# A hybrid streaming encoder step on one core: the gated projection with tokens on partitions, its result turned by VectorE, and VectorE and ScalarE held in source order beside it

## The chip, the core and the metric

The kernel runs on one core of a Trainium2 chip. A core has a matrix engine (TensorE, PE in the profile), a vector engine (VectorE, DVE), an activation engine (ScalarE, ACT), a general engine (GpSimd, POOL) and a queue that mostly issues transfers (SyncE, SP). Each engine takes its instructions in one fixed order and waits, at an instruction, until everything that this instruction needs is there; what stands behind it waits too. The metric is the device time of one execution in microseconds (us); three runs of the kernel before gave 1998.6, 1998.66 and 1998.87.

## The reference, cut to what matters

One layer of an encoder is applied to 384 frames in float32: 256 frames of a new stream and 8 running streams of 16 frames. With `h = rmsnorm(x)` and one combined projection `proj = h @ w_in` it computes

```
u  = glu_in[:, :1024] * sigmoid(glu_in[:, 1024:])          # gated input of the convolution
A  = swish(layernorm(causal_dwconv(u, 31 taps))) @ conv_pw_out
q, k = rmsnorm(q), rmsnorm(k) ; logf = log_sigmoid(f_logit)
B  = softmax(q k^T * scale + cumsum(logf) bias, causal) v @ w_att_out    # 8 heads of 128
x  = x + (sigmoid(gA) * A + sigmoid(gB) * B) @ w_out
x  = x + (silu(causal_dwconv(g, 3 taps)) * u2) @ w_down , [g | u2] = rmsnorm(x) @ w_up
```

It returns both outputs, the new keys, values and forget logs, and the new convolution states (the last 30 rows of `u` for each stream, the last two of `g`).

## The kernel before

**Products.** All large products run on PE in a split form: each float32 operand is written as `hi` (rounded to the matmul's input type) plus `lo` (the rest), and hi·hi, hi·lo and lo·hi are added up. The activations are split once. The weights are streamed by `fetch` through three raw buffers of 128 x 2 x 512, and each raw tile is split by `split_rows` (lines 146 to 149): ScalarE casts `hi` (L148), then VectorE subtracts `lo` (L149). There are three `hi`/`lo` pairs, so the ScalarE cast for weight tile n can start only when PE has read tile n-3 for the last time. `ahead` asks for the splits two or three tiles before PE needs them.

**Jobs and units.** `gemm` runs a list of jobs. One pass of its inner loop, called a *unit* here, is one 128-deep slice of the contraction; a weight tile serves two units. A job of kind "B" has the tokens on partitions: three token blocks, each 128 x 512 in PSUM, nine matmuls a unit (L250 to L252). A job of kind "A" has features on partitions: four blocks of 128 features by 384 tokens, twelve matmuls a unit (L245 to L247). Only the gated projection (4 jobs of 16 units, units 0 to 63 in what follows) is of kind "A". At the end of each unit `tick` runs work that was put off by `after` and then one step of each side generator; so side work is tied to units in the source.

**The stages.** Values, queries and keys come first, with RMS norms; then the gated projection, beside which the attention of all heads and the first part of the 31-tap convolution run; then the two gate projections (8 jobs of kind "B", 128 units), beside which the rest of the convolution and its layer norm run; then the projections of attention and convolution, `w_out`, and the feed-forward part (up and down), which takes from about 800 us to the end.

**Beside the gated projection.** For head h, `attention` puts these steps behind unit 5+6h+off: off 1 `head_operands` (VectorE turns the past keys, `kTs`, L611), off 4 `head_scores` (PE; then VectorE adds the bias and takes maxima, `pr`, L636; ScalarE exponentials L639, VectorE reciprocals, ScalarE scaling L641), off 9 `head_probs` (PE transposes; copies by ScalarE and VectorE), off 12 `head_out` (PE; copies `on` L665 and `attT` L670 by VectorE), off 14 `head_last` (PE transposes `on`). `conv` yields one step a unit: for channel block c the states are loaded, `fill` builds the shifted input `ext` (16 units apart for load, 3 before the first tap), and each of 31 taps is one VectorE instruction (L752 for the first, L754 for the rest) that works in place in `ut`. Blocks follow each other every 17 units, beginning 24 units after unit 0. `fill` also has PE transpose two pieces of `ut` (L740, L741), which ScalarE copies and SP stores as the new state; the first tap overwrites `ut`, so it waits for these transposes. The evacuation of a gated job (`glu_evac`) multiplies PSUM by the token scale `rs1b` laid along the free axis (L706, L710), takes the sigmoid on ScalarE and multiplies on GpSimd (L711).

**What sets the order.** PE's order is the source's. The other engines' order is made when the program is built, by a planner that models times and takes, of what is ready, what comes first in the source; `tc.high_priority(offset)` moves a piece of work forward by so many instructions: 150 for splits (`SPLIT_AHEAD`), 250 for attention steps (`ATT_AHEAD`), 400 for evacuations (`EVAC_AHEAD`), nothing for the convolution. `queued` chains an instruction behind the last one so chained on its engine. The result is one fixed list for each engine, whatever the chip then does.

## Time and profile before

| | us |
|---|---|
| median of three runs | 1998.66 |
| the profiled execution: its time | 1998.56 |
| its span in the profile | 1996.7 |
| gated projection: first to last of its matmuls | 214.6 to 384.7 |
| gates and what follows until 646 us | 261.2 |
| PE busy in the span | 1986.5 |

A row of a group gives line, engine, operation, tiles, shapes, count, then busy time and mean duration, then the idle time of the engine in front of these instructions and who ended it. A row of the timeline gives start and duration in us, then the same; where several instructions are merged, the count stands at the end. Matmuls are pipelined: each lasts longer than the distance to the next, so the pace is read from starts, and a wait of PE shows as a gap between starts.

### The profile page before, as it was taken

The page shows a single profiled execution, that of the slowest core. Times are in us where ns is not written, and L with a number is a line of the kernel's source. Part 1 is how long each engine was busy: PE and PEld are TensorE (multiplying, and loading weights), DVE is VectorE, ACT ScalarE, POOL GpSimd, SP SyncE. Part 2 cuts the span into 40 slices and gives each one's busy share as a digit, 9 for nine tenths or more (in the row PEclk, how much of TensorE's full clock was granted, in tenths as well). Part 3 has the DMA queues.
Part 4 walks back from the last instruction along what each step waited for, and adds up shares of the span by engine and source line. Part 5 has one row for each costly group of instructions (what it writes and reads, how often), then busy time and mean ns, then how long its engine had stood idle before and what let it go on. Part 6 is the DMA issues. An engine that isn't in the chain of part 4 may idle for free.

```text
span 1996.7 us, 24449 instructions
## 1 busy us (share of the span) xinstructions
PE 1986.5 (99%) x9383; PEld 1676.0 (84%) x9383; DVE 1305.3 (65%) x1908; ACT 743.2 (37%) x1077; POOL 89.5 (4%) x216
## 2 busy tenths in 40 slices
PE   9999999999999999999999999999999999999999
PEld 9888999888888888888888888888888888888887
DVE  4455889788755487676867683377673376638663
ACT  5535354433334433344333432233332233323321
POOL 1000011100000000000000000010000000000000
PEclk9999999999999999999999999999999999999999
DMA  6564767444443334534344443444433444343443
GB/s 184 149 188 117 216 154 161 141 140 131 130 129 124 128 125 163 165 122 137 119 137 126 129 134 129 129 126 127 136 129 132 132 118 137 128 133 120 138 158 106
DMA packets 209254, 275.98 MB, mean 138 GB/s; under 512 B 55878, under 2 KB 96729, under 8 KB 209129
## 3 DMA queue, kind: packets, MB, share of 16 engines
q1 hardware_dynamic: 208817, 273.85, 46.0%
q8 instruction: 73, 1.20, 0.3%
q0 software_dynamic: 288, 0.57, 0.1%
q14 instruction: 44, 0.36, 0.1%
q10 hardware_dynamic: 32, 0.01, 0.0%
HBM read 266.98 MB, written 7.86 MB: 138 GB/s over the span
## 4 chain that ended last, share of the span: by engine, by line
PE 96%; DVE 2%; DMA 1%; issue 0%; SPq 0%; ACT 0%; DVEq 0%; ACTq 0%
PE acc L252 20%; PE acc L250 20%; PE acc L251 20%; PE misc L252 10%; PE misc L251 10%; PE misc L250 10%; PE acc L245 2%; PE acc L247 2%; PE acc L246 2%; DVE lo L149 1%; DMA raw<-in_w_in_dram 0%; DVE mixT L267 0%; DVE ut L754 0%; DMA vc<-in_cache_v_dram 0%; DMA bs<-c_dr 0%
## 5 line engine op out<-in xcount | busy, mean ns | idle before, releaser
L149 DVE TENSOR_TENSOR lo<-raw,hi 128x1024 fp32r<-128x1024 f32 (+2 forms) x481 | 580.5, 1207 | 530.7 <-ACT hi L148 526.8
L148 ACT CAST hi<-raw 128x1024 fp32r<-128x1024 f32 (+2 forms) x481 | 496.3, 1032 | 970.1 <-PE misc L252 841.1
L250 PE MATMUL acc<-hi,xg 128*128 128x512 f32 x704 | 274.9, 390 | 0.0
L252 PE MATMUL acc<-hi,xg 128*128 128x512 f32 x704 | 273.9, 389 | 0.0
L251 PE MATMUL acc<-lo,xg 128*128 128x512 f32 x704 | 273.9, 389 | 0.0
L250 PE MATMUL acc<-hi,hT 128*128 128x512 f32 (+1 forms) x512 | 193.0, 377 | 0.5 <-ACT hT L297 0.5
L252 PE MATMUL acc<-hi,hT 128*128 128x512 f32 (+1 forms) x512 | 190.4, 372 | 0.2
L251 PE MATMUL acc<-lo,hT 128*128 128x512 f32 (+1 forms) x512 | 190.3, 372 | 0.0
L250 PEld LDWEIGHTS acc<-hi,xg 128*128 128x128 f32 x704 | 132.1, 188 | 28.4
L754 DVE SCALAR_TENSOR_TENSOR ut<-ext,cw,ut 128x384 f32<-128x384 f32 x240 | 151.9, 633 | 6.0
L252 PEld LDWEIGHTS acc<-hi,xg 128*128 128x128 f32 x704 | 132.1, 188 | 27.5
L251 PEld LDWEIGHTS acc<-lo,xg 128*128 128x128 f32 x704 | 132.2, 188 | 27.1
L252 PE MATMUL misc<-hi,xg 128*128 128x512 f32 x352 | 137.0, 389 | 0.0
L250 PE MATMUL misc<-hi,xg 128*128 128x512 f32 x352 | 137.0, 389 | 0.0
L251 PE MATMUL misc<-lo,xg 128*128 128x512 f32 x352 | 136.9, 389 | 0.0
L250 PE MATMUL acc<-hi,act 128*128 128x512 f32 x352 | 136.9, 389 | 0.0
L251 PE MATMUL acc<-lo,act 128*128 128x512 f32 x352 | 136.9, 389 | 0.0
L252 PE MATMUL acc<-hi,act 128*128 128x512 f32 x352 | 136.9, 389 | 0.0
L267 DVE STREAM_TRANSPOSE extf<-tok 32x384 f32<-32x384 f32 x176 | 100.3, 570 | 30.9 <-ACT tok L988 28.2
L267 DVE STREAM_TRANSPOSE uT<-tok 32x384 f32<-32x384 f32 x176 | 100.3, 570 | 29.7 <-ACT tok L988 26.9
L250 PEld LDWEIGHTS acc<-hi,hT 128*128 128x128 f32 x512 | 96.2, 188 | 16.1 <-ACT hT L297 1.0
L252 PEld LDWEIGHTS acc<-hi,hT 128*128 128x128 f32 x512 | 96.1, 188 | 15.7 <-DVE hT L298 0.7
(325 smaller groups left out, 3133.8 us busy)
## 6 DMA issues: line engine op xcount, KB each, us to landing
raw<-in_w_up_dram SPq DMA_DIRECT2D x176, 512.0 KB
raw<-in_w_in_dram SPq DMA_DIRECT2D x96, 512.0 KB
raw<-in_w_down_dram SPq DMA_DIRECT2D x88, 512.0 KB
raw<-in_w_in_dram SPq DMA_DIRECT2D x64, 256.0 KB
raw<-in_w_out_dram SPq DMA_DIRECT2D x32, 512.0 KB
raw<-in_w_att_out_dram SPq DMA_DIRECT2D x16, 512.0 KB
raw<-in_conv_pw_out_dram SPq DMA_DIRECT2D x16, 512.0 KB
raw<-in_w_in_dram SPq DMA_DIRECT2D x23, 344.0 KB
```

The lines of the kernel that those rows point to most:

```text
L148: queued(nc.scalar.copy(hi[:, k, :o], raw[:, k, :o]), first)
L149: queued(tt(lo[:, k, :o], raw[:, k, :o], f(hi[:, k, :o]), op=ALU.subtract), first)
L245: mm(o, hi[:, kk, s], ah, start=st, stop=False)
L246: mm(o, hi[:, kk, s], al, start=False, stop=False)
L247: mm(o, lo[:, kk, s], ah, start=False, stop=sp)
L250: mm(o, ah[:, s], hi[:, kk, :n], start=st, stop=False)
L251: mm(o, ah[:, s], lo[:, kk, :n], start=False, stop=False)
L252: mm(o, al[:, s], hi[:, kk, :n], start=False, stop=sp)
L267: nc.vector.transpose(put(a, slice(32 * b, 32 * b + 32)), src[32 * a:32 * a + 32, b])
L754: stt(o, v, wc, o, op0=ALU.mult, op1=ALU.add)
```

## The change: a gated projection with tokens on partitions

Kind "A" goes. The gated jobs become like all others, with 256 gate and 256 value columns in one 512-wide block. `glu_evac` then works by token block: one sigmoid on ScalarE straight from PSUM with the token scale as its scale, and one VectorE instruction that scales the value half and multiplies; the rows go to a new tile `ur`. `glu_done` turns `ur` into `ut` by VectorE transposes of 32 x 192, sixteen a job, four in each of the last unit of the job and the three after it. The new states are stored straight from `ur` by two transfers; the PE transposes, copies and small stores in `fill` go, and so do `rs1b`, its diagonals and its matmuls.

From the start of the gated projection to its end, every VectorE and ScalarE instruction that goes through the new `InOrder` wrapper is chained in source order (`chained`), but the splits and the evacuations are left free. The attention priority goes; the reciprocals of a head become one instruction a unit later (`head_scale`); key loads move two heads ahead, bias loads are issued by GpSimd instead of SP and with the value loads stand eight units behind the head's start. The convolution begins two units later. At the very start the first sample loads go to ScalarE's queue and the second `x_chunk` stands ahead of the second half of the first split; at the end the last output block is added and stored in two halves.

```diff
-CONV_FIRST, CONV_LAG = 24, 17
+CONV_FIRST, CONV_LAG = 26, 17
-SPLIT_AHEAD, ATT_AHEAD, EVAC_AHEAD = 150, 250, 400
+SPLIT_AHEAD, EVAC_AHEAD = 150, 400
...
+    class InOrder:
...
+                d = op(*a, **kw)
+                if chained:
+                    queued(d)
+                return d
...
     def split_rows(hi, lo, raw, o, k):
         first = in_first()
-        queued(nc.scalar.copy(hi[:, k, :o], raw[:, k, :o]), first)
+        held, chained[:] = chained[:], []
+        queued(act.copy(hi[:, k, :o], raw[:, k, :o]), first)
         queued(tt(lo[:, k, :o], raw[:, k, :o], f(hi[:, k, :o]), op=ALU.subtract), first)
+        chained[:] = held
...
-                    if j["kind"] == "A":
-                        o = ps[m][:, :NT]
-                        mm(o, hi[:, kk, s], ah, start=st, stop=False)
-                        mm(o, hi[:, kk, s], al, start=False, stop=False)
-                        mm(o, lo[:, kk, s], ah, start=False, stop=sp)
...
         split_rows(hi, lo, first, V_COLS[0][0][1], slice(0, 1))
         x_chunk(0)
         warm_up(FILL)
+        x_chunk(1)
         split_rows(hi, lo, first, V_COLS[0][0][1], slice(1, 2))
-        x_chunk(1)
...
     def load_b(h):
-        nc.sync.dma_start(bs[:, 0:P], c_dr[h, 0:P].partition_broadcast(P))
+        nc.gpsimd.dma_start(bs[:, 0:P], c_dr[h, 0:P].partition_broadcast(P))
...
+            for off, step in ((1, head_operands), (3, next_keys), (4, head_scores), (5, head_scale), (8, next_rest),
+                              (9, head_probs), (12, head_out), (14, head_last)):
...
     def glu_evac(g):
-        def ev(m, ps):
-            if m < 2:
-                tt(sgb[m][:], ps[:, :NT], rs1b[:], op=ALU.mult)
-                nc.scalar.activation(sgb[m][:], sgb[m][:], AF.Sigmoid)
-            else:
-                tt(u, ps[:, :NT], rs1b[:], op=ALU.mult)
-                nc.gpsimd.tensor_tensor(u, u, sgb[m - 2][:], op=ALU.mult)
+        def ev(t, ps):
+            sgb = p_att.tile([P, 256], F32, tag="sgb", bufs=2, name="sgb")
+            act.activation(sgb[:], ps[:, 0:256], AF.Sigmoid, scale=rs1[:, t:t + 1])
+            stt(ur[:, t, 256 * g:256 * (g + 1)], ps[:, 256:512], rs1[:, t:t + 1], sgb[:], op0=ALU.mult, op1=ALU.mult)
+    def glu_done(g):
+            for b in range(4):
+                after(b, lambda b=b: blocks(ur[:, :, 256 * g:256 * (g + 1)], by_feature(ut[:, 2 * g:2 * g + 2]), [b]))
...
         def fill(c):
-            tr(ps[:, :P], ut[:, c, 2 * P:], ident[:])
-            tr(ps[:32, P:2 * P], ut[:, c, 224:256], ident[:])
-            nc.scalar.copy(su[:, 0, :], ps[:, :P])
...
+    chained.append(True)
+    gemm([job(16, ha, glu_evac(g), done=glu_done(g)) for g in range(4)], [att_steps, conv_steps])
     drain(att_steps)
+    chained.clear()
...
-                tt(ys, ps[:], ys, op=ALU.add)
+                parts = [(0, 512)] if not last or n < 3 or t < 2 else [(0, 256), (256, 256)]
```

## The prediction

> **What bounds the kernel now.** I read the page first, then the pace of the matmuls, then stages by windows, and last the timeline around each wait of PE.

> ```profile
> span 1996.7 us, 24449 instructions
> PE 1986.5 (99%) x9383; PEld 1676.0 (84%) x9383; DVE 1305.3 (65%) x1908; ACT 743.2 (37%) x1077; POOL 89.5 (4%) x216
> PE 96%; DVE 2%; DMA 1%; issue 0%; SPq 0%; ACT 0%; DVEq 0%; ACTq 0%
> ...
> 214.61:384.84 170.23, 167.73 (x1192) 161.55 (x1191) 140.47 (x300) 77.89 (x146) 17.72 (x23) 0.99 0.64 164
> 384.84:646.00 261.16, 261.01 (x1160) 215.55 (x1160) 192.24 (x272) 97.71 (x131) 10.17 (x17) 1.00 0.46 133
> ...
> 215.68 0.33 PE L245 MATMUL acc<-hT,hi 128*128 128x384 f32 x1
> 225.21 0.33 PE L246 MATMUL acc<-hT,hi 128*128 128x384 f32 x1
> 1984.65 0.39 PE L250 MATMUL acc<-hi,act 128*128 128x512 f32 x1
> 1991.91 0.39 PE L252 MATMUL misc<-hi,act 128*128 128x512 f32 x1
> ```

> PE is the bound: the chain is PE for 96%. The window rows (length, then busy time of PE, PEld, DVE, ACT, POOL) are the gated projection and the gates with what follows until the layer norm. In the first VectorE is busy 140 of 170 us, in the second 192 of 261: it is the engine with the least room, and where its work stands in a bad order PE will wait for it. The pace of PE: 55 steps of 384 columns take 9.53 us, 0.1733 each; 32 steps of 512 take 7.26, 0.2269 each. One unit is 12 x 0.1733 = 2.08 us before and 9 x 0.2269 = 2.04 us after; a weight tile (two units) is 4.08 us.

> PE really waits once in the gated projection:

> ```profile
> 349.72 1.04 ACT L148 CAST hi<-raw 128x1024 fp32r<-128x1024 f32 x1 [1.47 <-PE acc L246]
> 350.80 1.22 DVE L149 TENSOR_TENSOR lo<-raw,hi 128x1024 fp32r<-128x1024 f32 x1 [1.26 <-ACT hi L148]
> 351.94 1.24 DVE L611 STREAM_TRANSPOSE kTs<-kc 128x1024 f32<-128x1024 f32 x1
> 353.23 0.64 PE L630 MATMUL misc<-kTs,qz 128*32 128x128 f32 x16 [2.50 <-DVE kTs L611]
> ...
> 354.46 0.52 PE L245 MATMUL acc<-hT,hi 128*128 128x384 f32 x1
> 357.34 0.52 PE L245 MATMUL acc<-hT,hi 128*128 128x384 f32 x1
> ```

> This is the pattern on which the whole forecast rests. The planned order put a split in front of something that PE needs at once. The split's buffer came free only when PE ended the unit (L246), ScalarE cast 1.08 us until VectorE could start, VectorE subtracted 1.14, then turned the keys, and PE stood 2.50 us. After it ten matmuls came 0.32 apart instead of 0.173: 1.5 more. This stop cost 4.0.

> **The change part by part.** *Gains.* (a) Matmuls of the gated jobs: 768 x 0.1733 = 133.1 become 576 x 0.2269 = 130.7: -2.4. (b) The state transposes leave PE:

> ```profile
> 403.02 0.39 PE L252 MATMUL misc<-hi,hT 128*128 128x512 f32 x1
> 403.25 0.27 PE L740 MATMUL misc<-ident,ut 128*128 128x128 f32 x1
> ...
> 403.70 0.40 PE L251 MATMUL acc<-lo,hT 128*128 128x512 f32 x1
> ```

> From 403.02 to 403.70 stand two ordinary steps, 0.45; the pair adds 0.23, eight pairs -1.8. (c) The `rs1b` matmuls, six records like these: -0.5 (0 to -0.8). (d) The stop above has its cause in an order that is planned anew: -4.0. (e) Start:

> ```profile
> 1.32 0.46 SPq L104 DMA_DIRECT2D xs<-in_x_sample_dram  x1
> 7.34 0.48 ACT L148 CAST hi<-raw 128x344 fp32r<-128x344 f32 x1 [1.58 <-DMA raw<-in_w_in_dram]
> 8.36 0.42 PE L250 MATMUL acc<-hi,hT 128*128 128x344 f32 x1 [0.46 <-ACT hT L297]
> ```

> PE waits for the second block of `hT`, which stands on ScalarE behind a cast that waits for a transfer; now it stands ahead, and two sample issues of 0.46 no longer sit ahead of that transfer on SP. I take -0.8, between 0 (the third weight tile, which is late anyway, gives it back) and -1.3. (f) The last add (0.69 us for 512 columns) and its store in halves: -0.2, 0 to -0.5. Sum of gains -9.7: 1998.6 - 9.7 = 1988.9.

> *Costs in the gated projection.* The prices are these rows (a 32 x 192 transpose is not in the trace: 0.38 by the line from 0.434 for 256 elements to 0.58, the step of 6 in 3.48, for 384; 0.29 if half of 0.58):

> ```profile
> L731 DVE STREAM_TRANSPOSE ext<-sc 128x256 f32<-128x256 f32 x4 | 1.7, 434 | 1.5 <-DMA sc<-in_state_conv_dram 1.4
> 771.59 3.48 DVE L267 STREAM_TRANSPOSE mixT<-sgA 32x384 f32<-32x384 f32 x6
> L665 DVE COPY on<-misc 128x128 f32<-128x128 f32 x8 | 2.3, 285 | 6.0 <-PE misc L663 6.0
> L670 DVE COPY attT<-misc 128x256 f32<-128x256 f32 x8 | 3.3, 419 | 0.5 <-PE misc L669 0.5
> L640 DVE RECIPROCAL mx<-mx 128x1 f32<-128x1 f32 x24 | 3.5, 150 | 2.5 <-ACT pr L639 2.5
> L641 ACT ACTIVATE pr<-pr,mx 128x256 f32<-128x256 f32 x16 | 8.0, 503 | 7.2 <-DVE mx L640 5.6 <-DVE mx L638 1.4
> 290.71 1.28 ACT L707 ACT_TABLE_LOAD   x1
> 294.27 1.05 ACT L707 ACTIVATE sgb<-sgb 128x384 f32<-128x384 f32 x2 [2.27 <-DVE sgb L706]
> 338.98 0.38 PE L659 MATMUL misc<-vt,pT 128*128 128x128 f32 x2
> 340.42 0.39 PE L669 MATMUL misc<-pT,vt 128*128 128x128 f32 x2
> ```

> In the changed program's built order I looked, on VectorE, for instructions that cannot start before PE ends some unit and stand ahead of one that PE needs right then. There are four.
> A, unit 19: ahead of head 0's `on` copy, which PE needs as soon as unit 19 ends, stand the split of tile 12 (its buffer is freed by unit 19), one reciprocal and four transposes of `ur`: 1.08 + 1.14 + 0.15 + 4 x 0.38 + 0.28 = 4.2 us of waiting.
> B, unit 31, the end of gated job 1: ahead of head 2's `on` copy stand the three evacuations of that job and the split of tile 16. ScalarE does two sigmoids of 0.5 and the cast of 1.05, VectorE the split 1.14, the third evacuation 0.42, a reciprocal, a tap 0.65 and the copy: 4.7. The table load (1.28) need not be added: at 290.71 it ran ahead of the wait, as here; if it does not, 6.0.
> C, unit 49: between the end of job 2 (unit 47) and head 5's `on` copy VectorE has three evacuations 1.26, a split 1.14, seven transposes 2.7, two taps 1.3, a reciprocal and the copy, behind a sigmoid: 7.3. PE has two units and the output matmuls of head 5 (338.98 to 340.6, 1.6): 5.7. Wait 1.6, up to 3 if the third exponential, now behind the sigmoids and a table load, holds the reciprocal.
> D, unit 53: the rest of the same lag meets the copy of head 6's probabilities that `head_out` needs, 1.3 by the same count, 0 to 3.
> A to D 11.8 (8 to 16). Slow matmuls after a stop, as after 353.23: 1.5 each for A and B, 3.0 (0 to 6). Together +14.8.
> [...]

> *Cost beside the gates.* Here the chain is off and taps are free. Before, each block's first tap waited for PE's transposes of `ut`, and this held VectorE to PE's units:

> ```profile
> 408.89 1.22 DVE L149 TENSOR_TENSOR lo<-raw,hi 128x1024 fp32r<-128x1024 f32 x1
> 410.03 3.23 DVE L754 SCALAR_TENSOR_TENSOR ut<-ext,cw,ut 128x384 f32<-128x384 f32 x5
> 413.18 1.22 DVE L149 TENSOR_TENSOR lo<-raw,hi 128x1024 fp32r<-128x1024 f32 x1
> 414.31 2.57 DVE L754 SCALAR_TENSOR_TENSOR ut<-ext,cw,ut 128x384 f32<-128x384 f32 x4
> 416.81 1.22 DVE L149 TENSOR_TENSOR lo<-raw,hi 128x1024 fp32r<-128x1024 f32 x1
> 417.94 3.89 DVE L754 SCALAR_TENSOR_TENSOR ut<-ext,cw,ut 128x384 f32<-128x384 f32 x6
> 421.75 1.22 DVE L149 TENSOR_TENSOR lo<-raw,hi 128x1024 fp32r<-128x1024 f32 x1
> ...
> 438.70 0.48 DVE L752 TENSOR_SCALAR ut<-ext,cw,col 128x384 f32<-128x384 f32 x1 [2.02 <-PE misc L741]
> ```

> A split with 5, 4, 6 taps takes 4.29, 3.63, 4.94 us: 1.01 + 0.655 for each tap. With five, VectorE already loses 0.2 us a tile to PE's 4.08, and makes it good in the pause of 2.02 that the transposes force. After the change no such pause is left. The built order packs taps without a break: between the splits of tile 39 and tile 71 stand 175 taps and 5 fills, 5.5 a tile. That is 32 x 1.01 + 175 x 0.655 - 5 x 0.14 (first taps are shorter) + 5 x 0.37 = 148 us, against 32 x 4.08 = 131 on PE. The splits come free two units before use, less cast and subtraction: 4.08 - 2.2 = 1.9 of slack. So PE loses 148 - 131 - 1.9 = 15 us there, a few tenths to 1.5 at each tile (12 if VectorE enters this stretch ahead, 20 if GpSimd's sums slow taps: 3 taps took 2.88 instead of 1.96 beside GpSimd). Later, with the taps done, nothing is given back: PE cannot run faster.

> ```profile
> 295.91 2.88 DVE L754 SCALAR_TENSOR_TENSOR ut<-ext,cw,ut 128x384 f32<-128x384 f32 x3
> ```

> Work that I cost at nothing: the copies and sigmoids of ScalarE (78 of 170 us busy); the bias loads, asked for eight units, over 21 us, ahead of their add, and GpSimd's queue behind them, which loses eight products; SP, which loses the 32 issues of the bias loads (four a head) and 14 small stores. If a bias load is late, `pr` waits and with it all of VectorE, chained.
> Sum: 1988.9 + 14.8 + 15 = 2018.7, so 2019. The profiled execution, 1998.56, is 0.1 from the median, 1998.66; no correction. Three runs lie within 0.3 us, so 0.2% (4 us) is ample for telling a change.

> **The rivals.** *Faster, 1989 (chance 0.14):* the lists bind less than I think. If the split buffers are free earlier than a tile's last matmul, A and B shrink to the sums without cast and split, and if a tile's VectorE work stays below 4.08 us (under 4.7 taps a tile instead of 5.5) the gates cost nothing. All gains stay. Against it: the stop at 350.35 is exactly this pattern, with its length.
> *Only one of the two stretches, 2004 (0.09):* VectorE enters the gates so far ahead that the lag never reaches PE, or the stops A to D are hidden.
> *A clock that falls again and again, 2031 (0.05):* small waits at every tile beside the gates bring the 0.32 pace back; eight times 1.5 is +12. Against it: waits of 0.3 to 0.5 elsewhere (8.36) show no such run.
> *Bias loads late, 2033 (0.05):* eight heads at 1.8 us. [...]

> **How the numbers follow.** The forecast, both stretches, has 0.67 and runs from 2008 (A to D 8, no slow clock, gates 12) to 2031 (16 + 6 + 20). The range for 8 in 10 takes in the second rival: 2002 to 2032. Faster by over 0.2%: 0.14. Within: the bottom of the second rival, 0.02. Slower: 0.84.

> **What would show it.** Right: PE gaps of about 4 us behind unit 19 and unit 31, ended by `on`; slow matmuls after each; none at head 7's keys; beside the gates PE waits ended by `lo`, and VectorE near 95% busy until the last tap, some 60 us earlier than before in units. Steps (a) and (b) show as 0.2269 and no L740 rows. Wrong: if VectorE is idle beside the gates, or a gap of PE ends with `pr` behind a bias transfer.

## The result, and the profile after

The changed kernel takes 2017.46 us (median of five runs, 2016.52 to 2018.93) against 1998.6 us before in the same series: 1.0099 times as long, 95% interval 1.0086 to 1.0113. The forecast was 2019, so the total was met, but not its parts: the gated projection lost nearly twice what was counted, and the gates lost almost nothing.

The top of the page of the changed kernel, with the shares of the chain that ended last:

```profile
span 2015.6 us, 24006 instructions
PE 1989.6 (99%) x9169; PEld 1651.6 (82%) x9169; DVE 1312.7 (65%) x1950; ACT 739.6 (37%) x1063; POOL 101.8 (5%) x240
PE 88%; DVE 9%; issue 2%; ACT 0%; DMA 0%; SPq 0%; DVEq 0%; ACTq 0%
```

VectorE does nearly the same amount of work as before (1312.7 us against 1305.3), and yet it now ends 9% of the chain instead of 2%. Windows say where. A row is a stretch, its length, the busy time of PE, PEld, DVE, ACT and POOL, and the granted clock; first the changed kernel (gated projection, gates), then the gates of the kernel before, whose gated projection stands in the prediction:

```profile
212.40:403.98 191.58, 173.51 (x994) 138.89 (x993) 137.38 (x301) 78.87 (x142) 23.13 (x41) 0.95 0.62 149
403.98:668.76 264.78, 263.95 (x1167) 217.73 (x1165) 205.34 (x317) 95.87 (x123) 12.88 (x17) 1.00 0.46 133
```
```profile
384.84:649.74 264.90, 264.75 (x1176) 218.64 (x1176) 195.98 (x278) 101.43 (x135) 10.17 (x17) 1.00 0.45 132
```

The gated projection took 170.23 us before and takes 191.58: 21.35 more, with PE idle for 18 us of the stage (191.58 less 173.51) and its clock at 0.95. The gates take 264.78 against 264.90. The projection starts 2.2 us earlier than before (212.40 against 214.61), and what follows the gates is the same within 0.2 us. So the loss lies in one stage. The waits of PE in it, by line, engine that ended them, sum, number and longest:

```profile
PE misc L688 <- DVE on L89: 9.1, 3, 4.4
PE misc L634 <- DVE pz L89: 5.0, 2, 3.2
PE misc L632 <- DVE attT L89: 3.2, 1, 3.2
PE misc L638 <- DVE qz L89: 0.8, 1, 0.8
```

(L89 is the wrapper through which every VectorE instruction now goes, so tiles tell them apart; L688 is the transpose of `on` in `head_last`, L632 and L634 are the second and third score product of a head, L638 its product with the past keys.) The wait behind unit 19, which the prediction called A, in the timeline:

```profile
259.57 0.39 PE L264 MATMUL acc<-hi,hT 128*128 128x512 f32 x1
259.99 1.04 ACT L89 CAST hi<-raw 128x1024 fp32r<-128x1024 f32 x1 [4.65 <-PE acc L264]
261.07 1.22 DVE L89 TENSOR_TENSOR lo<-raw,hi 128x1024 fp32r<-128x1024 f32 x1 [2.60 <-ACT hi L89]
262.21 0.17 DVE L89 RECIPROCAL mx<-mx 128x3 f32<-128x3 f32 x1
262.41 1.52 DVE L89 STREAM_TRANSPOSE ut<-ur 32x192 f32<-32x192 f32 x4
263.95 0.29 DVE L89 COPY on<-misc 128x128 f32<-128x128 f32 x1
264.38 0.30 PE L688 MATMUL misc<-ident,on 128*128 128x128 f32 x1 [4.43 <-DVE on L89]
```

Read it downwards: PE ends the unit, only then may ScalarE cast into the freed buffer, VectorE has stood idle for 2.60 us in front of the subtraction that needs the cast, and the 0.29 us copy that PE waits for stands behind all of it. 4.43 was measured, 4.2 was forecast. The second kind of wait was not foreseen. Unit 33, in the same view:

```profile
309.04 0.70 PE L632 MATMUL misc<-qt,attT 128*128 128x256 f32 x2
309.67 1.13 DVE L89 STREAM_TRANSPOSE ut<-ur 32x192 f32<-32x192 f32 x3
310.83 1.23 DVE L89 TENSOR_TENSOR lo<-raw,hi 128x1024 fp32r<-128x1024 f32 x1
312.09 0.37 DVE L89 STREAM_TRANSPOSE ut<-ur 32x192 f32<-32x192 f32 x1
312.47 0.29 DVE L89 COPY pz<-misc 128x128 f32<-128x128 f32 x1
312.91 0.76 PE L634 MATMUL misc<-qt,attT 128*128 128x128 f32 x2 [3.17 <-DVE pz L89]
```

The score product at L634 reads nothing that `pz` holds. It waits for a place to write: PSUM holds three `misc` tiles, a head's scores want all three, and the last of them still held probabilities of the head before, which VectorE copies out as `pz`.

### The profile page after: what moved, and what is told of

It reads as the page before. It is cut to its first block, busy times and chain, and to the rows that moved or that the text cites. A ratio compares the mean times of both kernels' runs of the same rounds, so it can differ in the third digit from the quotient of the medians.

```text
span 2015.6 us, 24006 instructions
## 1 busy us (share of the span) xinstructions
PE 1989.6 (99%) x9169; PEld 1651.6 (82%) x9169; DVE 1312.7 (65%) x1950; ACT 739.6 (37%) x1063; POOL 101.8 (5%) x240
## 4 chain that ended last, share of the span: by engine, by line
PE 88%; DVE 9%; issue 2%; ACT 0%; DMA 0%; SPq 0%; DVEq 0%; ACTq 0%
PE acc L262 20%; PE acc L263 20%; PE acc L264 20%; PE misc L264 9%; PE misc L262 9%; PE misc L263 9%; DVE ut L89 5%; DVE lo L89 3%; DVE mixT L89 0%; DVE sgA L89 0%; ACT hi L89 0%; PE misc L638 0%; PE misc L307 0%; PE misc L676 0%; DMA xs<-in_x_prompt_dram 0%
## 5 line engine op out<-in xcount | busy, mean ns | idle before, releaser
L89 DVE TENSOR_TENSOR lo<-raw,hi 128x1024 fp32r<-128x1024 f32 (+2 forms) x481 | 579.9, 1206 | 533.0 <-ACT hi L89 528.9
L89 ACT CAST hi<-raw 128x1024 fp32r<-128x1024 f32 (+2 forms) x481 | 495.7, 1031 | 961.2 <-PE misc L264 834.6
L262 PE MATMUL acc<-hi,hT 128*128 128x512 f32 (+1 forms) x704 | 272.9, 388 | 0.0
L263 PE MATMUL acc<-lo,hT 128*128 128x512 f32 (+1 forms) x704 | 267.9, 381 | 1.1 <-DVE lo L89 1.1
L264 PE MATMUL acc<-hi,hT 128*128 128x512 f32 (+1 forms) x704 | 267.6, 380 | 0.0
L263 PEld LDWEIGHTS acc<-lo,hT 128*128 128x128 f32 x704 | 133.8, 190 | 24.4 <-DVE lo L89 2.2
L262 PEld LDWEIGHTS acc<-hi,hT 128*128 128x128 f32 x704 | 133.7, 190 | 24.4 <-issue 2.1
L264 PEld LDWEIGHTS acc<-hi,hT 128*128 128x128 f32 x704 | 133.6, 190 | 23.5
L89 DVE SCALAR_TENSOR_TENSOR ut<-ext,cw,ut 128x384 f32<-128x384 f32 x240 | 138.2, 623 | 0.8
L89 DVE STREAM_TRANSPOSE extf<-tok 32x384 f32<-32x384 f32 x176 | 100.3, 570 | 30.9 <-ACT tok L89 28.2
```

What stands on the lines that cost most here:

```text
L89: d = op(*a, **kw)
L262: mm(o, ah[:, s], hi[:, kk, :n], start=st, stop=False)
L263: mm(o, ah[:, s], lo[:, kk, :n], start=False, stop=False)
L264: mm(o, al[:, s], hi[:, kk, :n], start=False, stop=sp)
```

## The experiments

The theories. *Theory 1*: PE loses time where a VectorE copy that it needs, as an operand or because the copy empties a PSUM tile, stands in the built list behind splits and transposes. *Theory 2*: the stage simply holds too much VectorE work. *Theory 3*: a convolution tap costs more when it reads what the tap just before it wrote. *Theory 4*, formed on the way: beside the gates PE loses by how densely the list is packed. Ratios are to the kernel before.

| run | time, us | ratio (95%) | gated projection, us | gates, us |
|---|---|---|---|---|
| before (1997.5 to 1998.6 in four series) | 1998 | 1 | 170.2 | 264.9 |
| changed | 2017.46 | 1.0099 (1.0086 to 1.0113) | 191.6 | 264.8 |
| e1, transposes spread | 2007.31 | 1.0049 (1.0033 to 1.0066) | 180.8 | 264.6 |
| e2, one PSUM tile less | 2009.0 | 1.0058 (1.0043 to 1.0073) | 183.1 | 264.7 |
| e3, not chained | 2002.93 | 1.0029 (1.0018 to 1.0040) | 178.8 | 263.4 |
| e4, bias by SP | 2019.55 | 1.0111 (1.0096 to 1.0126) | 191.2 | 264.7 |
| e5, taps in runs | 2015.45 | 1.0088 (1.0073 to 1.0104) | 191.5 | 262.3 |
| e6, splits in order | 2009.31 | 1.0056 (1.0040 to 1.0070) | 184.5 | 264.8 |
| e7, all places | 1995.5 | 0.9989 (0.9980 to 0.9997) | 164.9 | 267.8 |
| e8, e7 with free splits | 2007.73 | 1.0052 (1.0039 to 1.0066) | 180.5 | 263.7 |
| e9, e7 and e5 | 1993.56 | 0.9978 (0.9969 to 0.9987) | 165.6 | 265.0 |
| e10, e7 with queued taps | 1990.85 | 0.9966 (0.9954 to 0.9979) | 164.7 | 263.1 |

The last column needs one correction. In e7 to e10 twelve small matmuls of the layer norm come behind the end of the gates instead of in front of it, in e5 six. What follows the gates takes 1348.9 to 1349.1 us in e7 to e10 and 1347.6 in e5, against 1346.8 in the changed kernel; so some 2.0 and 0.8 us are to be added to their gates in a comparison.

**e1: the transposes of `ur` spread.**

```diff
-                after(b, lambda b=b: blocks(ur[...], by_feature(ut[...]), [b]))
+                after(2 * b, lambda b=b: blocks(ur[...], by_feature(ut[...]), [b]))
```

> Edit against the changed kernel: the four quarters of a job's ut transposes come two units apart instead of one. Same work on every engine, other places in VectorE's list. Theory 1 (places in the list: PE loses time where a copy that it or its PSUM buffers need stands behind splits and transposes): counted along the new built list with the durations of the trace, the wait behind unit 19 falls from 4.6 to about 2.8 us and so ends without its stretch of slow clock (about 1.7), the two waits at unit 33 lose 2 us in all, that at unit 51 some 2.5, and small ones of 0.5 to 1 come at the other heads: 5 to 7 us less, 2011 to 2013. Theory 2 (VectorE simply has too much work in this stage, 64 transposes of 0.37 us more, and PE pays for the sum wherever it stands): 2017, as the changed kernel.

10.2 us less than the changed kernel, with the same instructions. The waits of PE in e1:

```profile
PE misc L688 <- DVE on L89: 7.5, 3, 3.4
PE misc L634 <- DVE pz L89: 2.5, 4, 1.9
```

A is now 2.7 us instead of 4.4, and the waits of the score products fall from 8.2 us to about 3. Theory 2 alone can't explain the loss: the work is the same. The count was too careful by 4 us: the wait at unit 33, counted at about 1.2, came out at 0.15, and its half-clock stretch vanished too (the clock of the stage is 0.98 instead of 0.95); that behind A stayed against the count.

**e2: two score products in one PSUM tile.**

```diff
-        s1 = misc_tile()
-        mm(s1[:, :2 * P], qh[:, P:2 * P], kh[:, 0:2 * P], start=True, stop=True)
+        s1 = s0[:, P:]
+        mm(s0[:, P:3 * P], qh[:, P:2 * P], kh[:, 0:2 * P], start=True, stop=True)
```

> Edit against the changed kernel: the first two score products of a head (128 and 256 columns) share one PSUM tile, so a head asks for two of the three misc tiles at that place and not three. Theory 1 with the PSUM ring (the waits of 3.3 us at unit 33 and of 3.4 and 2.2 at unit 51 are waits for a misc tile that VectorE must empty first): these three go or move to the on copy of the same head; counted along the built list about 7 us less, near 2010, and 2008 if the clock keeps its pace there. If these waits had another cause (the query rows themselves, the keys, the bias), they stay: 2017.

As counted by theory 1. The waits of PE in e2:

```profile
PE misc L688 <- DVE on L89: 11.8, 3, 4.4
PE misc L680 <- DVE mx L89: 1.0, 1, 1.0
```

No wait of L632 or L634 is left: those 8.2 us were waits for a PSUM tile. VectorE's list had not become faster, and a part of the lag comes back at the next copy that PE needs (`on` 11.8 instead of 9.1 us).

**e3: the order not enforced.**

```diff
-    chained.append(True)
     gemm([job(16, ha, glu_evac(g), done=glu_done(g)) for g in range(4)], [att_steps, conv_steps])
```

> Edit against the changed kernel: the source order of VectorE and ScalarE beside the gated projection is not enforced; the planner places everything, the rest of the change stays. Theory 1: the list is another one and so are the waits; counted along it there are eight waits of 1 to 4.7 us, most of them now for a split that comes late (units 32 to 47) and none behind unit 19: about 8 us less than the changed kernel, 2009 to 2011, still slower than before. Rival (the enforced order alone is the loss): all waits go, and the gains stay: 1989 to 1992. Theory 2 (amount of work): 2017.

14.5 us less than the changed kernel and still slower than before; the count was 7 us too high. The planner's list makes other waits, for splits (0.5 us of the first row falls at the kernel's start, the rest in this stage):

```profile
PE acc L263 <- DVE lo L89: 7.6, 4, 3.6
PE acc L262 <- ACT hi L89: 1.2, 2, 0.7
```

VectorE is busy 159.8 us inside this shorter stage of 178.8 us, against 137.4 of 191.6 in the changed kernel: more work there and less time, which speaks against theory 2 once more.

**e4: bias loads issued by SP again.**

```diff
-        nc.gpsimd.dma_start(bs[:, 0:P], c_dr[h, 0:P].partition_broadcast(P))
+        nc.sync.dma_start(bs[:, 0:P], c_dr[h, 0:P].partition_broadcast(P))
...
```

> Edit against the changed kernel: SP issues the bias loads again, in the same places. Theory 1: no gain, 2017 to 2019 (SP then stands in front of weight loads, and the first heads' scaling comes a little later). [...]

Not faster: 1.0111 against 1.0099, with intervals that overlap. So GpSimd's issues don't explain the loss; nor does the profile of the changed kernel put any wait of PE or VectorE in this stage down to a bias load.

**e5: taps in runs of one block.** From unit 65 on, a window of eight steps gives eight taps of one block, then eight of the next, and the taps are queued:

```diff
+                d = stt(o, v, wc, o, op0=ALU.mult, op1=ALU.add)
+            if not chained:
+                queued(d)
...
+        for t in range(39, 7 * CONV_LAG + CW, 8):
+            for c in range(8):
+                for i in range(8):
+                    step(c, t + i)
```

> Edit against the changed kernel: from the end of the gated projection on, the convolution's taps are queued in runs of eight of one block, where the changed kernel alternates between two blocks; the same taps, operands and results. Theory 3 (a tap that reads the ut rows that the instruction just before it wrote starts later; that is why a tap took 0.654 us from start to start before and 0.529 after): by the built order 112 of 138 neighbouring taps beside the gates are then of one block, and these show 0.65, the others 0.53; PE loses nothing more, because the planner spreads the taps thinner and ends them some 55 us later: 2016 to 2019. Rival (GpSimd's traffic, the state copies or PE's transposes of ut made taps slow before, and these are gone): all taps stay at 0.53.

The pitch of taps between two splits: five taps of the changed kernel, where two blocks alternate, then four taps of one block in e5.

```profile
433.16 2.73 DVE L89 SCALAR_TENSOR_TENSOR ut<-ext,cw,ut 128x384 f32<-128x384 f32 x5
435.81 1.22 DVE L89 TENSOR_TENSOR lo<-raw,hi 128x1024 fp32r<-128x1024 f32 x1
```
```profile
472.76 2.57 DVE L89 SCALAR_TENSOR_TENSOR ut<-ext,cw,ut 128x384 f32<-128x384 f32 x4
475.25 1.22 DVE L89 TENSOR_TENSOR lo<-raw,hi 128x1024 fp32r<-128x1024 f32 x1
```

From tap to tap the median is 0.529 us in the changed kernel and 0.653 in most of e5's gates; where the changed kernel has one block left (from 560 us) it shows 0.654 too. In four taps only the last, in front of the split, costs 0.53: 3 x 0.653 + 0.53 is the 2.49 from 472.76 to 475.25. Theory 3 holds and its rival falls: the order alone makes the price. That it is the reading of `ut`, and not of another tile that neighbours of one block share, is the nearest explanation and was not separated. PE lost nothing by it, and the time came out just under the forecast: the gates became 2.5 us shorter, 0.8 of which returns behind them. The planner spread the taps until 623 us, and no wait for a split is left beside the gates.

**e6: the splits in source order too.**

```diff
-        held, chained[:] = chained[:], []
         queued(act.copy(hi[:, k, :o], raw[:, k, :o]), first)
         queued(tt(lo[:, k, :o], raw[:, k, :o], f(hi[:, k, :o]), op=ALU.subtract), first)
-        chained[:] = held
```

> Edit against the changed kernel: the splits too are held in source order beside the gated projection (there the split for a weight tile is asked for two tiles ahead, at a unit by which its buffer is free). Theory 1: the wait behind unit 19 falls from 4.6 to about 1 us, since no split stands there any more; the waits that come from the third evacuation at unit 31 (3.9) and from the transposes in front of the score tiles (3.1 at unit 33, 2.7 and 3.5 at 49 to 51) stay: 4 to 8 us less, 2009 to 2013. Theory 2 (amount of work): 2017.

8.2 us less, as counted. The waits of PE in e6 (its score products are L630 and L632, its transpose of `on` L686):

```profile
PE misc L632 <- DVE pz L89: 6.9, 3, 3.5
PE misc L686 <- DVE on L89: 3.6, 1, 3.6
PE misc L630 <- DVE attT L89: 2.4, 2, 1.6
```

A is gone, which was the split's; that at unit 31 and those for PSUM tiles stay.

**e7: every place changed, no instruction.** To e6 it adds:

```diff
-ATT_FIRST = 5
-CONV_FIRST, CONV_LAG = 26, 17
+ATT_FIRST = 4
+CONV_FIRST, CONV_LAG = 30, 17
...
-            ... (4, head_scores), (5, head_scale), ... (14, head_last)):
+            ... (5, head_scores), (6, head_scale), ... (15, head_last)):
...
-                after(b, lambda b=b: blocks(...
+                after(2 + 3 * b, lambda b=b: blocks(...
```

> Edit against the changed kernel: the same instructions in other places. Splits in source order too; a head starts a unit earlier but asks for its scores at offset 5 and for its last transpose at 15; the quarters of the ut transposes come 2, 5, 8 and 11 units behind the job; the convolution begins four units later. Theory 1: counted along the built list no wait of PE over 0.4 us is left beside the gated projection, so the 19.5 us of stops and the 8 to 9 of slow clock of the changed kernel go and its gains stay, less about 1 us for a later end of the convolution: 1990, from 1988 to 1993, below the kernel before. Theory 2: the work is the same, so 2010 to 2017. [...]

The gated projection takes 164.89 us, 5.3 less than before the change and 26.7 less than in the changed kernel, with a clock of 1.00 throughout. That is theory 1: the longest wait of PE left in the stage is 0.74 us. But the time is 1995.5, outside the forecast of 1988 to 1993: the gates take 3.0 us more than in the changed kernel, 5.0 with the correction above. Their window in e7, and then the only wait of PE in its first 182.9 us:

```profile
377.13:644.92 267.79, 264.55 (x1154) 215.53 (x1153) 207.50 (x313) 95.20 (x124) 11.20 (x17) 1.00 0.46 131
```
```profile
PE acc L261 <- DVE lo L89: 3.2, 7, 0.6
```

Seven waits for a split, each up to 0.6 us: a shape that the prediction had described for the changed kernel. VectorE is busy there for 174.7 of the 182.9 us.

**e8: e7 with the splits left free.**

```diff
+        held, chained[:] = chained[:], []
         queued(act.copy(hi[:, k, :o], raw[:, k, :o]), first)
         queued(tt(lo[:, k, :o], raw[:, k, :o], f(hi[:, k, :o]), op=ALU.subtract), first)
+        chained[:] = held
```

> Edit against e7: only the splits are left free again, as in the changed kernel; all else is as in e7. Theory 1: the planner then puts splits ahead of copies and exponentials that PE needs, as in the changed kernel; counted along the list there are six waits of 0.7 to 4.1 us, 11 to 12 us together: 2001 to 2004. If the splits' places don't matter, as e7.

12.2 us more than e7. The difference was counted as 11 to 12, from an e7 at 1990; as e7 itself came out at 1995.5, the forecast of 2001 to 2004 was missed. The waits of PE in e8, and the longest of them in the timeline:

```profile
PE misc L662 <- ACT pr L89: 6.6, 4, 3.7
PE misc L688 <- DVE on L89: 3.9, 1, 3.9
```
```profile
262.48 1.04 ACT L89 CAST hi<-raw 128x1024 fp32r<-128x1024 f32 x1 [2.84 <-DMA raw<-in_w_in_dram]
263.43 0.50 ACT L89 ACTIVATE pr<-pr,mx 128x256 f32<-128x256 f32 x1
263.99 0.33 PE L662 MATMUL misc<-ident,pr 128*128 128x128 f32 x1 [3.66 <-ACT pr L89]
```

So the free placing of the splits alone costs 12.2 of the 22.0 us between the changed kernel and e7: it puts a cast that comes late ahead of the scaling that PE waits for. In A the cast waited for PE; here it waited for its weight transfer.

**e9 and e10: e7 with the taps beside the gates queued,** in runs of eight (e9, the edit of e5) and in source order, where two blocks alternate (e10, only the `queued(d)` of e5).

> Edits of e7 and e5 together: e7's places, and beside the gates the taps queued in runs of eight of one block. In e7 the tiles beside the gates are over 4.08 us by 6 us in all, with VectorE busy 174.7 of the first 182.9 us there and waits ended by lo; in e5, where the queue makes the planner spread the taps until 623 us, the gates have no such tile. Theory 4 (what PE loses beside the gates is the density of VectorE's list, and a queue of taps thins it): the 6 us go although each neighbouring tap of one block costs 0.125 us more: 1989 to 1991. Rival (the price of a tap decides, not its place): 116 pairs at 0.125 us more cost VectorE 14.5 us and PE a part of it: 1996 to 2010.

> Edit against e7: the taps beside the gates are queued in source order, where they alternate between two blocks (neighbours of one block: 17 of 124), so that each stays at 0.53 us. Theory 4: the queue alone thins the list (the last tap comes near 602 instead of 553 us), so the 6 us go as in e9: 1989 to 1991. Rival (taps' price): a few us less than e9 and as fast as the price allows, while e9 is slower than e7.

The two windows of e10, gated projection and gates:

```profile
212.34:377.01 164.67, 163.85 (x995) 133.89 (x993) 131.81 (x292) 76.10 (x139) 22.21 (x41) 1.00 0.70 172
377.01:640.15 263.14, 262.24 (x1154) 216.29 (x1153) 208.12 (x313) 95.56 (x124) 9.14 (x17) 1.00 0.46 133
```

e10 meets the forecast of theory 4 and is the fastest kernel of the study, 0.34% below the kernel before. e9 misses the same forecast (1989 to 1991) and lies between e7 and e10: its taps cost 0.125 us more and end no later (609 against 614 us), its gates are 1.9 us longer, and it has one more wait of 1.1 us in the projection. So both density and price count, and theory 4 alone was too simple.

## Why the prediction was right, and where it was wrong

The time was right, its parts were not: two errors of some 14 us cancelled, and that is luck.

*What bounds the kernel* and *the pattern* (a copy that PE needs, behind a split that waits for PE): right. A was forecast at 4.2 and measured at 4.43. B was forecast at 4.7 and is 3.35: the first two sigmoids need not wait for the unit's end, since PE finishes token block after token block. In the timeline at unit 31:

```profile
297.62 0.48 ACT L89 ACTIVATE sgb<-acc,rs 128x256 f32<-128x256 f32 x1 [6.07 <-PE acc L264]
298.55 0.39 PE L264 MATMUL acc<-hi,hT 128*128 128x512 f32 x1
302.29 0.30 PE L688 MATMUL misc<-ident,on 128*128 128x128 f32 x1 [3.35 <-DVE on L89]
```

The first sigmoid starts 1.3 us before PE's last matmul ends (298.94). C was 1.6 and is 1.31. The old stop at head 7's keys is gone, as forecast.

*D and what was missing.* D (1.3 at unit 53) did not occur. In its place stand waits that the count had no line for: 3.17 at unit 33, 3.20 and 1.79 at unit 51, and 0.82 at unit 9 for head 0's `qz`. The failed step is "instructions that cannot start before PE ends some unit and stand ahead of one that PE needs right then": "needs" was read as operands only, and e2 shows that a free PSUM tile is a need too. All waits are 18.1 us instead of 11.8 (A to D).

*The slow clock* was forecast for A and B at 3.0. The stage lost 21.35 although it gained 2.4 by faster matmuls, 4.0 by the old stop and 0.7 by three pairs of state transposes: 28.4 in all. Less 18.1 of waits this leaves 10.3. Six windows of 3.41 us ran at a granted clock of 0.50, one after A, one after B, one at unit 33 and three from unit 51 on; at half the pace over their whole length, an estimate, they cost 10.2. So the term was too small in both: a window costs 1.7 and not 1.5, and there were six and not two.

*The gates* were forecast to lose 15. They lose 1.0: 264.78 against 264.90, where five of the eight pairs of state transposes stood, 1.15 by the prediction's price. Two waits for `lo` make it, 0.37 at 543.52 and 0.31 at 560.44, each 0.5 from start to start of the matmuls. VectorE is as full as forecast, 154.4 busy of the first 156.0 us, and the built order does hold 5.5 taps a tile. The term that failed is the price of a tap: 0.654 was read from rows where each tap works on the tap before it, and the changed order alternates two blocks, so 0.529 holds. With it the split's step is 1.14, for the 1.01 came from rows whose last tap already cost 0.53. 32 x 1.14 + 175 x 0.529 + 5 x 0.37 = 131 us, as much as PE's 131. The trace shows 135 for these 32 tiles (from 423.99 to 559.17); where the other 4 went was not taken apart, and PE lost only 1.0 of them. The longest tile of taps alone has seven:

```profile
537.40 1.22 DVE L89 TENSOR_TENSOR lo<-raw,hi 128x1024 fp32r<-128x1024 f32 x1
538.54 3.79 DVE L89 SCALAR_TENSOR_TENSOR ut<-ext,cw,ut 128x384 f32<-128x384 f32 x7
542.24 1.22 DVE L89 TENSOR_TENSOR lo<-raw,hi 128x1024 fp32r<-128x1024 f32 x1
543.52 0.50 PE L263 MATMUL acc<-lo,hT 128*128 128x512 f32 x1 [0.37 <-DVE lo L89]
```

These 4.84 us against PE's 4.08 stand right ahead of the first of the two waits. e7 and e9 show that the mechanism itself is real when more taps fall into the gates. One sign of the prediction failed with the price: the last tap was to come some 60 us earlier; it comes 165.5 us behind the start of the gates instead of 184.3, so 19 earlier.

*The gains.* Start and `rs1b` were taken at -1.3 and are -2.2. The tail is -0.2, as forecast. The rival *bias loads late* falls with e4. No run shows its 1.8 us a head: in the changed kernel only GpSimd waits in this stage for these transfers, 19.9 us in seven waits, and neither PE nor VectorE does. *Only one of the two stretches* had the place right, and its 2004 fails because the stops in that stretch were counted too small. *Faster, 1989* is what e10 reaches with other places (1990.85): the gains were there, and the changed list hid them.

## What to carry over

Where the order of an engine is a fixed list, price a change by walking that list: for every instruction that the bottleneck engine waits for, find what stands ahead of it that itself waits for the bottleneck, and count PSUM tiles and other buffers among the needs. Hold such late-released work (here the splits) to a place where its buffer is already free, and move it before one removes any work: e7 and e10 differ from the changed kernel in places alone, by 22 and 27 us. And take the price of an instruction from a row with the same neighbours, not only the same shape.

## What the runs showed of the hardware that was not expected

**An in-place chain cost a quarter more in these runs.** Taps of 128 x 384 last 0.61 us each. They follow each other in 0.529 us when they alternate between two blocks and in 0.654 when each reads what the one before wrote, with the same instruction (changed kernel and e5). At 0.529 each tap starts 0.08 us before the one ahead of it ends, at 0.654 it starts 0.04 us behind that end: working on the result of the tap just before cost 0.125 us a tap.

```profile
315.97:319.38 3.41, 1.05 (x3) 0.67 (x4) 3.37 (x7) 2.04 (x3) 0.00 (x0) 1.00 0.78 178
319.38:322.79 3.41, 3.41 (x11) 2.72 (x10) 2.73 (x3) 0.00 (x0) 0.00 (x0) 0.50 0.77 229
```
```profile
260.62:264.04 3.42, 1.60 (x8) 0.98 (x6) 0.67 (x1) 1.74 (x4) 0.95 (x4) 1.00 1.09 367
264.04:267.45 3.41, 1.61 (x8) 1.38 (x9) 3.28 (x9) 0.40 (x2) 0.00 (x0) 1.00 0.58 181
267.45:270.86 3.41, 3.41 (x20) 2.87 (x19) 1.88 (x5) 0.59 (x1) 0.00 (x0) 1.00 0.32 53
```

In e3 PE was idle for 2.36 us of one window, and the next ran at 0.50. In e4 it was idle for longer, 3.62 us, but spread over two windows with 1.60 and 1.61 us busy, and the clock stayed at 1.00. So in these traces the busy time of a window went with the clock of the next, and the idle time alone did not. This was read from the traces only, not tried by an experiment, and what sets the length of a half-clock stretch was not worked out.
